# Turning two of four frame columns on VectorE by way of memory in a streaming encoder step

## The chip, the core and the metric

The kernel runs on one core of a Trainium2 chip. Its time is the device time of one execution in microseconds, from the first instruction to the last with what lies around them. A core has five engines that work side by side, each with a queue of its own: TensorE (PE in the profile; its weight loads are PEld), VectorE (DVE), ScalarE (ACT), GpSimd (POOL) and SyncE (SP), whose queue here issues most transfers. An engine works its queue in order, so an instruction that waits stops those behind it.

## What is computed

One layer of an encoder over 2048 new frames and 32 more frames of a running stream, 1024 wide. Cut to what matters:

```python
hn = rmsnorm(h, g_mix)
hA, bA, cA, zA, vB, zB = split(hn @ w_in)             # six times 512 columns
u  = cA * hA
yA = bA * (causal_conv3(u) + conv_b) * silu(zA)
pooled = trailing_mean(vB, windows 2, 4, 8, 16) - vB  # a window for each group of 128 channels
yB = (per_group(pooled) @ pool_w) * pool_scale * silu(zB)
h  = h + concat(yA, yB) @ w_out
gate = sigmoid(rmsnorm(h, g_ple) @ w_ple_gate)
y  = rmsnorm(h + (p @ w_ple) * gate, g_final)
```

`pool_w` has four matrices of 128 x 128, one for each group.

## The kernel before, in words

**Precision.** Every operand of a large product is kept as two parts, a high part (a copy to fp32r by ScalarE, L78) and a low part, the source minus the high part (VectorE, L79). `split` makes both. A product takes three matmuls for each block of the contraction: high by high, high by low, low by high.

**Frames.** The 2080 frames stand in five blocks of 416 (`NB`). Blocks 0 and 1 are the first group, 2 and 3 the second, 4 the third (`GROUPS`, L26). A block is cut into columns: three of 128 frames (c = 0, 1, 2) and one of 32 (c = 3). For a group of two blocks a column holds two tiles of 128 frames, or, for c = 3, one tile with 2 x 32 frames.

**Seven products for eight.** For two blocks and two weights at once the kernel forms sums and differences of the frames' quarters (names 11, 21, T1, T2, T3, 22, T4) and of the weights' quarters, and takes seven half products (`half_product`, L560) where eight would be due. A product is 12 matmuls of 128 x 416. `Unit.pair` (L859) issues the seven in order, in three PSUM banks X, Y and Z: product 1, 3, 5 and 7 in X, 2 in Y, 4 and 6 in Z. Between two products in one bank an engine takes the intermediate sum out: ScalarE by `carry` (L871), VectorE by `out` (L874). The fifth product's sum is taken by VectorE, and the seventh product then goes on in the same bank.

**Units.** A unit is a group and one of four blocks of 128 channels (`Unit`, L674). Units 0 to 3 belong to the first group, 4 to 7 to the second, 8 to 11 to the third. Unit 0 and the third group's units are computed plainly (`plain`, L777), the others with three pairs of weights: zb and v, c and h, za and b (`seven`, L899). v goes into the pooling mixer: `pool_blocks` (L731) takes the trailing mean, `mix` (L719) multiplies it with the unit's pooling weights (three matmuls per block, L724 to L726, into a PSUM bank). In `seven` the mix follows the second pair, in the third group it follows the product h directly.

**The second group's frames** are prepared while units 1 to 3 compute. `next_columns(3, 0, 1, 2)` (L1047) is a generator that does a column in small steps. `at_pace` (L1115) runs it beside the products: `aside` is called at each of the eight steps of a pair (24 times in a unit), and every call is worth 39/62 of a generator step. For a column `frame_sums` (L437) does this:

- the mean square of every tile, on ScalarE (`x_stat`, L397, L89), and the reciprocal root on GpSimd (L70, L74);
- the scaling of every tile with root and gain, one VectorE instruction a tile (`normal`, L404, L407);
- for each half of the 1024 rows, transposes on TensorE into a PSUM bank (`turn`, L411, L416), four for each tile. They are held in the written order;
- a copy of two of the quarters to SBUF by ScalarE (L452, L459), and four differences on VectorE (L449);
- for each of the seven names a `split` into a staging tile and a transfer to HBM from GpSimd's queue (`to_memory`, L483, L488).

When units 1 to 3 are done, `load_group` (L498, L502) brings the seven tiles of the second group back from HBM, seven transfers of 1664 KB.

**The last block** (block 4) takes another way (`last_block`, L1059), beside units 5 to 7. `scaled_to_memory` (L1091) scales a tile in four VectorE instructions, each writing 256 of 1024 columns in another order (L1098), and writes it to `xs_d` in HBM from GpSimd's queue (L1100). `from_memory` (L1102) reads it back in four transfers on SP's queue (L1106), each of which puts blocks of 32 frames on 32 partitions. `turned_in_place` (L1110) then transposes blocks of 32 x 32 in place, one VectorE instruction for the tile (L1112). After this the frames lie in the free dimension, as after a full transpose; TensorE takes no part.

**Rings.** Frame tiles, scaled tiles and staging tiles share the ring `xin`, five slots of 4 KB a partition (L337). The raw weights have the ring `raws`, four slots (L334). The pooling weights of all four groups are loaded once into a slot of that ring (L668, L669), and split once behind unit 0's first block (`vectors`, L656, L660).

**Order of the work.** A planner puts the instructions of each engine's queue in order by their place in the program and by its own estimate of when their inputs are ready. It may put a later instruction in front of an earlier one that would wait. `tc.keep_in_program_order` holds an instruction behind those that are written before it.

Of the kernel before, what the change touches and what calls it, by code (L numbers as in the profile page):

```python
# [9 lines left out]
F32 = mybir.dt.float32  # L10
F32R = mybir.dt.float32r
# [4 lines left out]
P = 128  # L16
D = 1024
# [13 lines left out]
LATE = 2  # L31
LATER = 4


@with_exitstack
def trunk(ctx, tc, x_p, x_s, c_conv, c_pool, p_p, p_s, g_mix, w_in, conv_w, conv_b, pool_w,
# [30 lines left out]
    def rstd_of(ssq, n, name, r=None):  # L67

        ms = sm.tile([P, 1], F32, tag="ms", name=f"ms_{name}")
        nc.gpsimd.tensor_scalar(ms[:n], ssq[:n], scalar1=1.0 / D, scalar2=EPS,  # L70
                                op0=ALU.mult, op1=ALU.add)
        if r is None:
            r = sm.tile([P, 1], F32, tag="rstd", name=f"rstd_{name}")
        nc.gpsimd.tensor_tensor(r[:n], ms[:n], nhalf[:n], op=ALU.pow)  # L74
        return r
# [255 lines left out]
    with ExitStack() as s1:  # L331
# [4 lines left out]
        frames_in = ExitStack()  # L336
        xin = frames_in.enter_context(tc.tile_pool(name="xin", bufs=5, side="right"))  # L337
        big = pool("big", 1)
# [134 lines left out]


        NAMES = ("11", "21", "T2", "T1", "T3", "22", "T4")
        SLOTS = (("11", "21"), ("T2", "T1"), ("T3", "22"))
# [6 lines left out]
        def to_memory(mem, name, src, at, n, t=None, later=False):  # L483
            t = t or staged(name)[:, :, :, :n]
            ins = put(t, src)
            if later:
                tc.keep_in_program_order(ins)
            nc.gpsimd.dma_start(mem[:, :, :, at:at + n], t.bitcast(F32))  # L488
# [156 lines left out]
        vec = const.tile([P, 112], F32, name="vec")  # L645
        pw = one.tile([P, 2, 4, P], F32R, name="pw")
        rows = ftile("rows").rearrange("p k n -> p (k n)")[:112, :P]
# [8 lines left out]
        def vectors():  # L656
            pv = tbank("pv")
            tc.keep_in_program_order(nc.tensor.transpose(pv[:, :112], rows, ident[:112, :112]))
            nc.vector.tensor_copy(vec, pv[:, :112])
            split(pw[:, 0], pw[:, 1], pw_raw)  # L660

# [5 lines left out]

        pw_raw = raws.tile([P, 4, P], F32, tag="t", name="raw_pw")  # L668
        nc.sync.dma_start(pw_raw, pool_w[0].rearrange("g c d -> c g d"))  # L669

# [3 lines left out]
        class Unit:  # L674


            def __init__(self, gi, tbs, j):
                self.gi, self.tbs, self.j, self.tag = gi, tbs, j, f"{gi}_{j}"
                self.L = min(SEQ - tbs[0] * NB, len(tbs) * NB)
                self.last = tbs[-1] == 4  # L680
                self.pooled = None
                t = lambda name, n: big.tile([P, n], F32, tag=name, name=f"{name}_{self.tag}")

                own = (gi, j) != (1, 0)
                self.zs = t("zs", 2 * NB) if own else ring4(xin, f"zs_{self.tag}")
                self.V = t("V", 2 * NB + 16)
                self.U = t("U", 2 * NB + 4)
                self.c_s = t("c_s", 2 * NB) if own else ring4(xin, f"c_s_{self.tag}")
                self.history(self.V, 15, halo_v, hist_v(j))
# [25 lines left out]
            def store(self, chunk, b, t):  # L715
                r = self.tbs[b] * NB
                nc.sync.dma_start(y_d[chunk, :, r:r + NB], self.cols(t, b))

            def mix(self, b):  # L719

                pp, j = self.cols(self.pooled.rearrange("p h n -> p (h n)"), b), self.j
                pq = self.pooled[:, 1, b * NB:b * NB + NB]
                pm = tbank(f"pm_{self.tag}_{b}")
                nc.tensor.matmul(pm[:, :NB], pw[:, 0, j], pp, start=True, stop=False)  # L724
                nc.tensor.matmul(pm[:, :NB], pw[:, 0, j], pq, start=False, stop=False)
                nc.tensor.matmul(pm[:, :NB], pw[:, 1, j], pp, start=False, stop=True)  # L726
                z = self.cols(self.zs, b)
                nc.vector.scalar_tensor_tensor(z, pm[:, :NB], pscale(j), z, op0=ALU.mult, op1=ALU.mult)
                self.store(4 + j, b, self.zs)
# [169 lines left out]
            def seven(self, B, aside, both=False):  # L899
# [54 lines left out]
                while i < 3:  # L954
# [4 lines left out]
                    for n in range(8):  # L959
# [3 lines left out]
                        if n == (0 if both else LATER):  # L963
                            while i and late:
                                tc.keep_in_program_order(split(*late.pop()))
                        if both and i == 2 and n == 3:
                            for b in range(2):
                                self.mix(b)
# [78 lines left out]
        def next_columns(*cs):  # L1047

            load_ahead(1, cs[0])
            for c, after in zip(cs, cs[1:] + (None,)):  # L1050

                places = iter(t[:, :, :, i * DEC:(i + 1) * DEC] for t in map(staged, ("short_0", "short_1")) for i in range(4))
                dst = lambda q, src, n: to_memory(p_d[q], f"{q}_1_{c}", src, c * P, n, next(places) if n == DEC else None, True)
                for i, _ in enumerate(frame_sums(ahead.pop((1, c)), f"g1_{c}", dst)):
                    if after is not None and i in (6, 7):
                        load_half_ahead(after)
                    yield
# [30 lines left out]

        xs_d = tc.dram_tile([NB, D], F32, name="xs_d")

# [37 lines left out]
        for gi, tbs in enumerate(GROUPS):  # L1128
# [17 lines left out]
            for j in range(4):  # L1146
                unit = gi * 4 + j
                u = Unit(gi, tbs, j)
                if unit == 0:
# [3 lines left out]
                    p_d["T4"] = tc.dram_tile([P, KH, 2, NB], F32, name="p_dT4b")  # L1153
                    aside = at_pace(next_columns(3, 0, 1, 2), 39, 62)
                elif gi == 0:
# [446 lines left out]
```

## Time and profile before

| | |
|---|---|
| median of three runs | 926.43 us (925.31 to 927.96) |
| profiled execution | 927.1 us |
| its span, first to last instruction | 925.3 us |
| mean granted clock of TensorE | 0.994 |
| instructions | 12917 |
| moved to and from HBM | 186.37 MB, mean 201 GB/s |

The profile is of a single execution on the chip. Its page gives, for each engine, the time in which it was busy; the span in 40 equal slices with the busy share of each in tenths; the transfers; and the costliest groups of instructions by line of the program, with the number of instructions, the mean duration, and what ended the idle time in front of them. The trace behind it also answers who waited for whom, and lists instructions in order of time. Instructions of one engine overlap, so that the distance between two starts says more of the cost of an instruction than its own duration. In the rows, `x12` is a number of instructions, `128x512 f32` partitions x elements and type, and `[0.87 <-DVE U L874]` an idle time of 0.87 us that ended with the VectorE instruction of line 874 on tile U.

### The profile page before, as it was taken

What the parts mean: (1) busy time and instruction counts of PE and PEld (TensorE: products, weight loads), DVE (VectorE), ACT (ScalarE), POOL (GpSimd) and SP (SyncE); (2) the same over time, 40 slices, a digit from 0 to 9 for tenths busy, and PEclk for the clock granted to TensorE, in tenths of its full rate; (3) what the DMA queues carried; (4) which work ended last, traced back from release to release, by engine and by line L of the source; (5) the groups of instructions that cost most, each with busy time, mean ns of one, the idle gap of its engine ahead of it and who ended that gap; (6) DMA issues with size and microseconds to landing.
All of it is one profiled execution on the core that took longest, in us unless ns stands there. A gap on an engine that the chain in (4) does not pass through costs nothing. (4 is left out here: it accounts for less than half of the span.)

```text
span 925.3 us, 12917 instructions
## 1 busy us (share of the span) xinstructions
PE 907.0 (98%) x4479; PEld 819.9 (89%) x4479; DVE 722.8 (78%) x1225; ACT 476.2 (51%) x880; POOL 152.8 (17%) x276
## 2 busy tenths in 40 slices
PE   7999999999999999999999999999999999999996
PEld 5999999999999999999999987888877868888884
DVE  6896898999488989785777679665554799888965
ACT  6744556554345455443545456334334776565554
POOL 3110222312001111000000010111111002333324
PEclk8999999999999999999999999999999999999998
DMA  8345555859955646357755359756775886799882
GB/s 245 87 152 153 167 160 178 265 154 317 411 165 174 191 155 189 100 180 277 201 169 173 125 192 289 263 186 177 251 220 167 292 259 160 190 232 232 227 240 91
DMA packets 140654, 186.37 MB, mean 201 GB/s; under 512 B 12044, under 2 KB 111244, under 8 KB 139309
## 3 DMA queue, kind: packets, MB, share of 16 engines
q1 hardware_dynamic: 120093, 126.07, 44.4%
q0 software_dynamic: 17760, 53.97, 19.8%
q10 hardware_dynamic: 2736, 5.51, 1.8%
q8 instruction: 35, 0.57, 0.3%
q14 instruction: 30, 0.25, 0.1%
HBM read 128.93 MB, written 56.56 MB: 200 GB/s over the span
## 5 line engine op out<-in xcount | busy, mean ns | idle before, releaser
L78 ACT CAST y_S<-y_fS 128x512 fp32r<-128x512 f32 x32 | 19.5, 621 | 41.9 <-PE x_o L168 18.9
L103 PE MATMUL e<-wq,pps 128*128 128x512 f32 (+1 forms) x156 | 38.9, 399 | 0.2 <-ACT pps L78 0.2
L168 PE MATMUL x_o<-wo_b,y_S 128*128 128x512 f32 x128 | 35.8, 391 | 0.0
L168 PE MATMUL x_g<-wg_b,g_S 128*128 128x512 f32 x128 | 35.7, 389 | 0.0
L564 PE MATMUL x_zbv<-B,w_zbv_S 128*128 128x416 f32 x168 | 34.2, 352 | 0.0
L564 PE MATMUL x_zab<-B,w_zab_S 128*128 128x416 f32 x168 | 34.1, 351 | 0.0
L564 PE MATMUL x_ch<-B,w_ch_S 128*128 128x416 f32 x168 | 34.1, 351 | 0.0
L564 PE MATMUL z_zab<-B,w_zab_S 128*128 128x416 f32 x168 | 34.0, 351 | 0.0
L564 PE MATMUL z_zbv<-B,w_zbv_S 128*128 128x416 f32 x168 | 34.0, 351 | 0.0
L564 PE MATMUL z_ch<-B,w_ch_S 128*128 128x416 f32 x168 | 34.0, 350 | 0.0
L103 PEld LDWEIGHTS e<-wq,pps 128*128 128x128 f32 (+1 forms) x156 | 27.4, 182 | 6.9 <-ACT pps L78 0.5
L1391 POOL DMA_DIRECT2D e<-h_d x28 | 24.8, 907 | 52.3 <-DVE e L1388 45.3
L70 POOL TENSOR_SCALAR ms_x<-ssq_x 128x1 f32<-128x1 f32 (+2 forms) x18 | 10.7, 592 | 127.5 <-ACT junk L89 127.2
L564 PEld LDWEIGHTS z_zbv<-B,w_zbv_S 128*128 128x128 f32 x168 | 31.4, 188 | 0.3
L564 PEld LDWEIGHTS z_zab<-B,w_zab_S 128*128 128x128 f32 x168 | 31.4, 188 | 0.3
L564 PEld LDWEIGHTS z_ch<-B,w_ch_S 128*128 128x128 f32 x168 | 31.4, 188 | 0.3
L564 PEld LDWEIGHTS x_zab<-B,w_zab_S 128*128 128x128 f32 x168 | 31.3, 188 | 0.4
L564 PEld LDWEIGHTS x_ch<-B,w_ch_S 128*128 128x128 f32 x168 | 31.3, 188 | 0.3
L564 PEld LDWEIGHTS x_zbv<-B,w_zbv_S 128*128 128x128 f32 x168 | 31.3, 188 | 0.4
L78 ACT CAST y<-y 128x512 fp32r<-128x512 f32 x24 | 14.8, 619 | 29.6 <-PE x_o L168 14.0
L168 PEld LDWEIGHTS x_o<-wo_b,y_S 128*128 128x128 f32 x128 | 23.9, 188 | 5.2 <-ACT c_o L1194 0.3
L168 PEld LDWEIGHTS x_g<-wg_b,g_S 128*128 128x128 f32 x128 | 24.0, 188 | 5.0
(582 smaller groups left out, 2649.9 us busy)
## 6 DMA issues: line engine op xcount, KB each, us to landing
y<-y_d SPq DMA_DIRECT2D x16, 512.0 KB, 6.3
x<-in_x_prompt_dram SPq DMA_DIRECT2D x16, 512.0 KB, 5.5
h_d<-x SPq DMA_DIRECT2D x16, 512.0 KB, 2.6
hn<-h_d SPq DMA_DIRECT2D x61, 128.0 KB, 6.7
xt<-in_x_prompt_dram SPq DMA_DIRECT2D x15, 512.0 KB, 7.4
e<-e_d SPq DMA_DIRECT2D x15, 512.0 KB, 5.9
e<-h_d POOLq DMA_DIRECT2D x28, 256.0 KB, 6.8
out_dram<-e POOLq DMA_DIRECT2D x14, 512.0 KB, 3.9
```

What stands on the lines that cost most here:

```text
L70: nc.gpsimd.tensor_scalar(ms[:n], ssq[:n], scalar1=1.0 / D, scalar2=EPS, op0=ALU.mult, op1=ALU.add)
L78: ins = nc.scalar.copy(hi, src)
L103: nc.tensor.matmul(ps[:n], pps[:, a, k, :n], wp[k][b][:, cs], start=k + q == 0, stop=k == 1 and q == 2)
L168: nc.tensor.matmul(ps[:n], lhs[:, k, a, :n], w[b][:, k], start=start and k + q == 0, stop=k == KH - 1 and q == 2, skip_group_check=True)
L564: nc.tensor.matmul(ps[:, :NB], lhs[:, k, x], b[:, k, y], start=start and k + q == 0, stop=stop and k == KH - 1 and q == 2, skip_group_chec ...
L1391: nc.gpsimd.dma_start(ee, h_d[r:r + P, at[1] * NH:at[1] * NH + NH], accum_op=ALU.add)
```

## The change

A new generator, `frame_blocks`, does for columns 3 and 0 what `frame_sums` does for a column; columns 1 and 2 keep `frame_sums`. It takes the last block's way: scaling in four pieces and a write to memory, four reads, one transpose in place. The quarters are then views of the transposed tile in SBUF, so the two ScalarE copies are not there, and the four differences and seven splits read SBUF. It has one step more than `frame_sums`, and the pace goes from 39/62 to 41/62 of a step a call. `xs_d` has rows for all these frames. The next column's two loads move from steps 6 and 7 to steps 8 and 9 (7 and 8 for column 3).

The ring `xin` gets a sixth slot of 4 KB. Pooling weights are loaded by every unit for its own group (128 x 128, in tiles of their own, one slot each), and split when the unit needs them: in `seven` behind the split of the pooled values, otherwise in `mix`. The tile of the mean square (`ms`) has four slots where it had eight.

```diff
+IN_BLOCKS = 3, 0
...
-        ms = sm.tile([P, 1], F32, tag="ms", name=f"ms_{name}")
+        ms = sm.tile([P, 1], F32, tag="ms", bufs=4, name=f"ms_{name}")
...
-        xin = frames_in.enter_context(tc.tile_pool(name="xin", bufs=5, side="right"))
+        xin = frames_in.enter_context(tc.tile_pool(name="xin", bufs=6, side="right"))
...
+        whole = lambda t: t.rearrange("p k (g t) -> p k g t", t=32)
+
+        def frame_blocks(xs, tag, rows, dst):
+            xs = [x_stat(x, True) for x in xs]
+            yield
+            for x, r in zip(xs, rows):
+                scaled_to_memory(x, r)
+                yield
+            ts = [from_memory(r, x[1]) for x, r in zip(xs, rows)]
+            yield
+            n = P if len(xs) == 2 else DEC
+            f1, f2, f3, f4 = (whole(ftile(f"f{c}_{tag}")[:, :, :n]) for c in range(1, 5))
+            sub = lambda o, x, y: nc.vector.tensor_tensor(o, x, y, op=ALU.subtract)
+            u = turned_in_place(ts[0])
+            p11, p21 = u[:, :KH, :n // DEC], u[:, KH:, :n // DEC]
+            dst("11", p11, n)
+            yield
+            if len(xs) == 2:
+                u = turned_in_place(ts[1])
+            else:
+                u = u[:, :, 1:]
+            p12, p22 = u[:, :KH], u[:, KH:]
+            sub(f1, p12, p11)
+            dst("T1", f1, n)
+            yield
+            sub(f2, p22, f1)
+            sub(f3, p22, p12)
+            dst("21", p21, n)
+            yield
+            sub(f4, p21, f2)
+            dst("22", p22, n)
+            yield
+            dst("T2", f2, n)
+            yield
+            dst("T3", f3, n)
+            yield
+            dst("T4", f4, n)
+            yield
...
-            ins = put(t, src)
+            v = whole if len(src.shape) == 4 else lambda a: a
+            ins = split(v(t[:, :, 0]), v(t[:, :, 1]), src)
...
-        pw = one.tile([P, 2, 4, P], F32R, name="pw")
...
-            split(pw[:, 0], pw[:, 1], pw_raw)
...
-        pw_raw = raws.tile([P, 4, P], F32, tag="t", name="raw_pw")
-        nc.sync.dma_start(pw_raw, pool_w[0].rearrange("g c d -> c g d"))
...
+                self.pw = one.tile([P, 2, P], F32R, tag="pw", name=f"pw_{self.tag}")
+                self.pw_raw = one.tile([P, P], F32, tag="pr", name=f"pr_{self.tag}")
+                nc.sync.dma_start(self.pw_raw, pool_w[0, j])
+                self.pw_whole = True
...
+            def pool_weights(self):
+                if self.pw_whole:
+                    self.pw_whole = False
+                    split(self.pw[:, 0], self.pw[:, 1], self.pw_raw)
+
             def mix(self, b):
+                self.pool_weights()
+                pw = self.pw
...
-                nc.tensor.matmul(pm[:, :NB], pw[:, 0, j], pp, start=True, stop=False)
+                nc.tensor.matmul(pm[:, :NB], pw[:, 0], pp, start=True, stop=False)
...
                                 tc.keep_in_program_order(split(*late.pop()))
+                                self.pool_weights()
...
-                for i, _ in enumerate(frame_sums(ahead.pop((1, c)), f"g1_{c}", dst)):
-                    if after is not None and i in (6, 7):
+                rows = (NB + c * P, 2 * NB + c * P) if c < 3 else (3 * NB,)
+                steps, loads = (frame_blocks(ahead.pop((1, c)), f"g1_{c}", rows, dst), (6 + len(rows), 7 + len(rows))) \
+                    if c in IN_BLOCKS else (frame_sums(ahead.pop((1, c)), f"g1_{c}", dst), (6, 7))
+                for i, _ in enumerate(steps):
+                    if after is not None and i in loads:
                         load_half_ahead(after)
...
-        xs_d = tc.dram_tile([NB, D], F32, name="xs_d")
+        xs_d = tc.dram_tile([4 * NB, D], F32, name="xs_d")
...
-                    aside = at_pace(next_columns(3, 0, 1, 2), 39, 62)
+                    aside = at_pace(next_columns(3, 0, 1, 2), 41, 62)
```

More of the change, by code (lines that the diff above doesn't have):

```diff
@@ L723, in mix @@
                 pm = tbank(f"pm_{self.tag}_{b}")
-                nc.tensor.matmul(pm[:, :NB], pw[:, 0, j], pp, start=True, stop=False)
-                nc.tensor.matmul(pm[:, :NB], pw[:, 0, j], pq, start=False, stop=False)
-                nc.tensor.matmul(pm[:, :NB], pw[:, 1, j], pp, start=False, stop=True)
+                nc.tensor.matmul(pm[:, :NB], pw[:, 0], pp, start=True, stop=False)
+                nc.tensor.matmul(pm[:, :NB], pw[:, 0], pq, start=False, stop=False)
+                nc.tensor.matmul(pm[:, :NB], pw[:, 1], pp, start=False, stop=True)
                 z = self.cols(self.zs, b)
```

## The prediction

> **What bounds the kernel now.** I read the busy times of the page first, then its forty slices, then the waits of TensorE in the stretch where the change acts, then the stretch unit by unit.
>
> ```profile
> span 925.3 us, 12917 instructions
> PE 907.0 (98%) x4479; PEld 819.9 (89%) x4479; DVE 722.8 (78%) x1225; ACT 476.2 (51%) x880; POOL 152.8 (17%) x276
> PE   7999999999999999999999999999999999999996
> DVE  6896898999488989785777679665554799888965
> ```
>
> TensorE (PE) is busy for 907.0 of 925.3 us, and only the first and last slices are not full. So a microsecond that TensorE no longer works is a microsecond of time, unless another engine makes it wait. The one with least room is VectorE (DVE): a slice is 23.1 us, and slices 4 to 10 (92 to 231 us), where the second group's frames are prepared, show 8 or 9 tenths.
>
> ```profile
> PE x_ch L564 <- DVE U L874: 0.9, 1, 0.9
> 78.47:129.26 50.79, 50.79 (x275) 49.52 (x275) 42.81 (x75) 27.48 (x55) 11.36 (x14) 1.00 0.49 147
> 129.26:181.84 52.58, 51.71 (x284) 50.61 (x283) 48.97 (x80) 30.54 (x58) 15.32 (x20) 1.00 0.78 240
> 181.84:232.66 50.82, 50.82 (x275) 49.74 (x274) 48.54 (x84) 26.93 (x50) 10.00 (x14) 1.00 0.76 235
> ```
>
> The first row is the only wait of TensorE between 40 and 320 us: 0.9 us for VectorE. The three others are units 1, 2 and 3 of the first group (stretch, its length, then busy us of PE, PEld, DVE, ACT, POOL, the granted clock, the DMA share, GB/s). VectorE works 42.81, 48.97 and 48.54 us in them: 140.3 of 154.2 us, 91%, with 13.9 us idle. The clock is 1.00, so nothing here is throttled.
>
> **What the change removes from TensorE.** Columns 3 and 0 lose their transposes on TensorE: 8 with 64 frames, 16 with 128. What a transpose costs is read from the starts of the products around it, not from its own duration, because instructions overlap. In the order of time (start, busy):
>
> ```profile
> 78.47 2.43 PE L564 MATMUL x_zbv<-B,w_zbv 128*128 128x416 f32 x12
> ...
> 87.63 0.46 PE L416 MATMUL pt_g<-ident,xt 64*128 64x64 f32 x4
> ...
> 95.02 0.46 PE L416 MATMUL pt_g<-ident,xt 64*128 64x64 f32 x4
> ...
> 97.78 2.43 PE L564 MATMUL y_ch<-B,w_ch 128*128 128x416 f32 x12
> ...
> 117.04 2.43 PE L564 MATMUL x_zab<-B,w_zab_S 128*128 128x416 f32 x12
> ...
> 121.58 1.04 PE L416 MATMUL pt_g<-ident,xt 128*128 128x128 f32 x8
> ...
> 124.72 2.43 PE L564 MATMUL z_zab<-B,w_zab_S 128*128 128x416 f32 x12
> 126.99 2.43 PE L564 MATMUL x_zab<-B_T,w_zab 128*128 128x416 f32 x12
> 129.26 1.03 PE L416 MATMUL pt_g<-ident,xt 128*128 128x128 f32 x8
> ...
> 132.40 2.43 PE L564 MATMUL y_zbv<-B,w_zbv 128*128 128x416 f32 x12
> ```
>
> A product of twelve matmuls starts 2.27 us after the one before it (124.72, 126.99, 129.26). From 117.04 to 132.40 there are six products, 13.62 us, and two sets of eight transposes: 15.36 - 13.62 = 1.74 us for column 0. From 78.47 to 97.78 there are eight products, 18.16 us, and column 3's two small sets: 19.31 - 18.16 = 1.15 us. Together **2.9 us** leave TensorE's own stream. Columns 1 and 2 keep theirs.
>
> ```profile
> L416 PE MATMUL pt_g<-ident,xt x56: 222/272/273, 87.6 to 199.4; 128*128 128x128 f32 x48, 64*128 64x64 f32 x8
> ```
>
> A single transpose has a duration of 272 ns, but eight cost 0.87 us, 0.11 us each: the rest lies beside neighbours. The Trainium skill (TensorE: Matmul & The Clock Gate, Part 4: PE-mode transpose) gives about 275 ns for a transpose inside a kernel. The trace has the same duration; a sum by it would take 24 times 0.275, an estimate of 6.6 us, off TensorE, and the spacing of the products speaks against that sum.
>
> **What it adds to VectorE.** These are the rows of what goes (L407, L459) and, from the last block, which already takes the way through memory, of what comes (L1098, L1112):
>
> ```profile
> L407 DVE SCALAR_TENSOR_TENSOR xt<-xt,rstd_x,g_bc 128x1024 f32<-128x1024 f32 (+1 forms) x14 | 18.0, 1283 | 9.6 <-POOL rstd_x L74 9.4 <-DVE g_bc L377 0.2
> 289.60 1.67 DVE L1098 SCALAR_TENSOR_TENSOR xs<-xt,rstd_x,g_bc 128x256 f32<-128x256 f32 x4 [0.73 <-POOL rstd_x L74]
> L1112 DVE STREAM_TRANSPOSE xb<-xb x4: 433/1232/1234, 303.6 to 380.2; 128x1024 f32<-128x1024 f32 x3, 128x256 f32<-128x256 f32 x1
> L459 ACT COPY f_g<-pt_g x4: 272/580/590, 95.5 to 200.5; 128x512 f32<-128x512 f32 x3, 128x128 f32<-128x128 f32 x1
> ```
>
> A full tile's scaling was one instruction of 1.28 us; it becomes four pieces, 1.67 us, and one transpose of 1.23 us. Column 0 has two tiles: 2 x (1.67 + 1.23 - 1.28) = 3.24 us. Column 3 has one tile of 64 rows: its pieces are as long per row, its transpose spans 512 elements, between 0.43 us (256) and 1.23 us (1024), so about 0.70 us by a straight line: 1.67 + 0.70 - 1.28 = 1.1 us. The four differences and seven splits of a column stay, as many and as wide, but read SBUF where they read PSUM; I take that as equal. So VectorE gets **4.3 us** more. ScalarE loses the two copies per column, 2 x 0.58 + 2 x 0.27 = 1.7 us; it has 40% idle here, so that is worth nothing.
>
> Pooling weights: one split of 512 columns becomes twelve of 128.
>
> ```profile
> L78 ACT CAST pw<-raw_pw x1: 622/622/622, 29.5 to 29.5; 128x512 fp32r<-128x512 f32 x1
> L79 DVE TENSOR_TENSOR pw<-raw_pw,pw x1: 680/680/680, 33.5 to 33.5; 128x512 fp32r<-128x512 f32 x1
> L79 DVE TENSOR_TENSOR short<-pt_g,short x3: 281/285/291, 89.6 to 100.2; 128x128 fp32r<-128x128 f32 x3
> 45.60 0.35 PE L724 MATMUL pm<-pp,pw 128*128 128x416 f32 x1
> ...
> 469.61 4.70 PE L564 MATMUL h<-hn,w_h 128*128 128x416 f32 x24
> 474.15 0.35 PE L724 MATMUL pm<-pp,pw 128*128 128x416 f32 x1
> ```
>
> Each costs VectorE 0.28 us, 0.84 us in units 1 to 3, and ScalarE about as much. In the third group TensorE goes from product h straight to the mix (474.15 is 4.54 us after 469.61), so a split that is done late would be seen. In the kernel before it was done 12 us ahead of the first mix (33.5 against 45.6 us); its inputs are in place a unit ahead, and both engines have gaps, so I cost it at nothing. If that cover is gone it costs up to 2.5 us a unit (a rival below).
>
> Put together: VectorE has 140.3 + 4.3 + 0.8 = 145.4 us of work in units 1 to 3, and these shrink to 154.2 - 2.9 = 151.3 us: 96% instead of 91%, 5.9 us idle instead of 13.9. It still fits, but only if nearly all of today's idle time can be used.
>
> **The way through memory, and the queues.**
>
> ```profile
> 291.56 0.60 POOL L1100 DMA_DIRECT2D xs_d<-xs  x1 [2.00 <-DVE xs L1098]
> 294.71 1.76 SPq L1106 DMA_DIRECT2D xb<-xs_d  x4
> xs_d<-xs POOLq DMA_DIRECT2D x3, 512.0 KB, 3.0
> xb<-xs_d SPq DMA_DIRECT2D x12, 128.0 KB, 2.7
> 100.36 0.37 SPq L514 DMA_DIRECT2D raw_zbv_2b<-in_w_in_dram  x1
> 108.95 0.68 DVE L542 TENSOR_TENSOR s_zbv<-raw_zbv_2b 128x512 f32<-128x512 f32 x1
> ```
>
> Three writes join POOL's queue, ahead of the next column's statistics, and twelve reads SP's. From the start of a tile's scaling to the tile back in SBUF: 1.67 + 0.60 + 3.0 + 1.76 + 2.7 = 9.7 us. A unit calls the generator 24 times in some 49 us and each call takes 41/62 of a step, so a step lasts 3.1 us. In column 0 the transpose stands three steps behind the scaling, 9.3 us: 0.4 us short. In column 3 it stands two steps behind, 6.2 us: 3.5 us short. The planner may put other ready work in front, but where it doesn't, a waiting transpose stops all of VectorE behind it: the sums that free PSUM banks (L874) and the low halves of weights (L79). On SP the reads wait for the write, with the next weights queued behind; such a weight tile was sent for at 100.36 and first read at 108.95, so a hold of some 4 us (the write's landing and its issue) stays hidden. The sixth ring slot lets loads start earlier, and TensorE waits for no such load today: nothing. DMA has a share of 0.49 in unit 1, where most of the extra transfers fall.
>
> The Trainium skill (SBUF — State Buffer, the warning on DVE blocking DMA) says that a DMA issued by GpSimd cannot get its descriptors while VectorE runs in a two-port mode; that would lengthen the write in this chain. The row above has 0.60 us for the issue and 3.0 us for the landing beside a busy VectorE, so the trace shows no such hold.
>
> **What I take for the new waits.** Their bounds: from below -1.0 us (today's one stall goes as well), from above everything that VectorE gains plus the two shortfalls, 4.3 + 0.8 + 3.9 = 9.0 us, if none is absorbed. The nearest row is that stall:
>
> ```profile
> 160.47 0.54 PE L564 MATMUL x_zab<-B,w_zab 128*128 128x416 f32 x2
> 161.89 2.55 PE L564 MATMUL x_ch<-B_T,w_ch 128*128 128x416 f32 x12 [0.87 <-DVE U L874]
> 161.26 0.58 DVE L874 TENSOR_TENSOR U<-x_ch,U 128x416 f32<-128x416 f32 x1
> ```
>
> The fifth product of a pair ends in bank X, VectorE must take it out (L874), and the seventh product needs the bank, one product later. So TensorE waits where VectorE is more than about 2 us late; here it was. Two matmuls (0.38 us) from 160.47 would have led to 160.85; the product started at 161.89, 1.0 us later. With VectorE at 96%, I take one more stall of this size: +0.9 us. The sum is -2.9 + 0.9 = **-2.0 us**. The profiled execution took 927.1 us, 1.8 of it outside the span, and lies 0.7 above the median of 926.4. Taken from the median: 924.4 us, 0.2% less. A measurement of this kernel can tell about 0.3%, 2.8 us, from no change, so the forecast is inside that.
>
> **The rivals.**
>
> ```profile
> DVE xt L407 <- POOL rstd_x L74: 4.8, 4, 3.4
> DVE w_zbv_S L79 <- ACT w_zbv_S L78: 3.8, 2, 2.3
> ```
>
> 1. Full gain. VectorE uses its idle time, and the stall at 161.9 stays or goes: -2.9 to -3.9 us, 923.5 to 922.5. For it: 8.6 us of VectorE's idle time between 60 and 240 us are waits for POOL and ScalarE (the rows above), which shrink by themselves when it runs late, and its weight work runs ahead (s_zbv at 108.95 is for a pair that starts at 130). Against it: today a stretch at 93% already gave a stall. Chance 0.30.
>
> 2. VectorE becomes the bound (the slower side). Place: units 1 and 2, at the sums from bank X. It decides where VectorE is over one product, 2.27 us, behind at such a sum; column 3's shortfall of 3.5 us alone does that. With half of the 9.0 us on the path: -2.9 + 4.5 = +1.6 us, 928.0; with all: +6.1 us, 932.5. For it: 96%, and the short way in column 3. Against it: 8.0 us of idle in unit 1, where column 3 and most of column 0 fall. Chance 0.22, half of it above +2.8 us.
>
> 3. The pooling split is left where it is written, behind the convolution. Then the mix in each of the third group's four units waits for VectorE's product and ScalarE's pass after h, some 2.5 us: -2.9 + 10.0 = +7.1 us, 933.5. Against it: the 12 us of lead. Chance 0.05.
>
> 4. Transposes cost their whole duration: 16 x 0.272 + 8 x 0.222 = 6.1 us, 920.3. The spacing of products speaks against it: 0.03. This is what the rule on transposes in the Trainium skill's TensorE page would come to.
>
> The forecast (-0.9 to -2.8 us) has 0.40.
>
> **How the numbers follow.** Faster by over 0.3%: rivals 1 and 4, 0.33. Slower by over 0.3%: rival 3, half of rival 2 and a little for the order of other work changing, 0.18. Within: 0.49. The range 922.4 to 929.0 takes in the forecast, rival 1 and the nearer half of rival 2; some 0.17 is left out. The forecast's own range is 923.6 to 925.5.
>
> **What would show it.** TensorE's transposes pt_g fall from 56 to 32, and products around columns 3 and 0 start 2.27 us apart; if TensorE's stream shortens by another amount than 2.9 us, the first term is wrong. VectorE's busy time in units 1 to 3 should be near 145 us. The waits of TensorE on VectorE (L874) before 235 us should add up to about 2 us; none means rival 1, over 5 means rival 2, with waits of the new transposes for the reads. A mix that waits for the low half of pw means rival 3. The prediction would be wrong most easily if the order of VectorE's queue elsewhere changed and stalls came or went in stages that the change doesn't touch.

## The result and the profile after

The changed kernel takes 938.21 us (median of five, 937.64 to 940.16) where the kernel before, on the same chip, takes 927.56 (925.31 to 927.96): a ratio of 1.0126 (of the means), 95% interval 1.0111 to 1.0142. It is slower by 1.3%, 10.7 us between the medians. The forecast was 924.4, with a range up to 929.0. The profiled execution took 940.16 us and was the slowest of the five. These are its span, its busy times, and TensorE's share and granted clock in forty slices:

```profile
span 938.4 us, 12956 instructions
PE 912.5 (97%) x4455; PEld 820.9 (87%) x4455; DVE 728.7 (78%) x1248; ACT 476.9 (51%) x887; POOL 153.4 (16%) x279
PE   7999998799999999999999999999999999999996
PEclk8999999899999999999999999999999999999998
```

The span is 13.1 us longer, while TensorE has 24 instructions fewer. TensorE's row has fallen in two slices, the seventh and eighth (141 to 188 us, 8 and 7 tenths), and the clock's in the eighth. The waits of TensorE between 100 and 260 us (us in total, times, longest), and then units 1, 2 and 3 (from the first product of a unit to that of the next, columns as in the prediction):

```profile
PE x_zab L610 <- DVE w_zab L80: 4.7, 1, 4.7
PE z_ch L610 <- ACT U L925: 2.2, 1, 2.2
PE x_ch L610 <- ACT c_s L925: 1.3, 1, 1.3
PE pt_g L417 <- DVE xt L408: 0.3, 1, 0.3
```

```profile
78.15:126.84 48.69, 48.69 (x259) 48.22 (x258) 42.93 (x84) 25.88 (x51) 11.72 (x16) 1.00 0.65 194
126.84:191.28 64.44, 55.89 (x275) 52.90 (x275) 53.35 (x86) 32.53 (x61) 16.11 (x21) 0.92 0.70 208
191.28:241.68 50.40, 50.40 (x276) 49.86 (x275) 48.33 (x83) 26.77 (x49) 10.09 (x15) 1.00 0.78 240
```

Unit 1 is 2.1 us shorter than before (48.69 against 50.79), unit 3 0.4 us shorter, and unit 2 11.9 us longer (64.44 against 52.58). VectorE is not full in unit 2: 53.35 of 64.44 us. Followed product by product, the second pair's third product starts at 147.22 where it started at 150.53: 3.3 us **ahead**. Unit 3 starts at 191.28 instead of 181.84: 9.4 us **behind**. So 12.7 us are lost in between. The four waits are 8.5 us, against 0.9 us in the kernel before. The rest, some 5 us, is for the most part a lower clock:

```profile
140.00:160.00 20.00, 16.18 (x82) 14.81 (x81) 15.12 (x26) 10.72 (x20) 6.87 (x10) 0.97 0.77 233
160.00:180.00 20.00, 15.27 (x66) 13.88 (x66) 18.11 (x29) 7.65 (x14) 2.58 (x3) 0.78 0.46 134
```

0.97 and 0.78 of the full clock over 20 us each are 0.6 + 4.4 = 5.0 us. In the kernel before, both stretches are at 1.00. In shorter stretches the clock is at half: 0.53 from 158.5 to 161.3, 0.50 from 161.4 to 162.0, and 0.50 from 173.5 to 178.5. From 171.0 to 173.5 (0.76) TensorE had no work, so 0.6 of the 5.0 us cost nothing: an estimate of 4.4 us for slower matmuls, and some 0.7 of the 12.7 us stay open. The clock's share also differs from one execution to the next. Two runs shown below with nearly the same waits (the one with 128 unused bytes and the one that reads back into the frame's own tile, 9.1 and 9.2 us) have 0.98 and 0.85, and 1.00 and 0.83, in these two stretches: 3.4 us each.

The chain that led there, from the changed kernel's timeline (start, duration, engine, instruction, and in brackets the idle time before it and what ended it):

```profile
144.93 2.91 SPq L394 DMA_DIRECT2D xt<-in_x_prompt_dram  x2
...
151.10 0.62 ACT L79 CAST T<-f_g 128x512 fp32r<-128x512 f32 x1 [3.05 <-DMA p_d<-21_1_0_1415]
...
152.68 0.48 ACT L925 COPY c_s<-x_ch 128x416 f32<-128x416 f32 x1
...
156.36 1.06 ACT L90 ACTIVATE junk<-xt 128x1024 bf16<-128x1024 f32 x1 [3.20 <-DMA xt<-in_x_prompt_dram]
...
157.42 0.49 ACT L925 COPY U<-z_ch 128x416 f32<-128x416 f32 x1
...
158.44 2.48 DVE L408 SCALAR_TENSOR_TENSOR xt<-xt,rstd_x,g_bc 128x1024 f32<-128x1024 f32 x2 [3.12 <-POOL rstd_x L75]
...
172.81 1.28 DVE L80 TENSOR_TENSOR w_zab<-raw_zab_2a,w_zab 128x512 fp32r<-128x512 f32 x2
...
173.54 3.84 PE L610 MATMUL x_zab<-B,w_zab 128*128 128x416 f32 x10 [4.73 <-DVE w_zab L80]
```

Read from the top: column 1's frames are asked for at 144.93. ScalarE, which has to keep the written order of these instructions, stops at 148 for a staging slot (the transfer of 21 has not landed), and at 153 for the second of the late frame tiles. Behind each stop stands a `carry` (c_s, U) that frees a PSUM bank, and TensorE waits for both. VectorE then scales column 1 from 158.44 on (from 149.85 in the kernel before), takes its quarters out, and only after these makes the low halves of w_zab, at 172.81. TensorE waits 4.73 us for them, and its next ten matmuls take 3.84 us (2.14 us for ten of them in the kernel before). The same places in the kernel before:

```profile
131.50 0.37 SPq L393 DMA_DIRECT2D xt<-in_x_prompt_dram  x1
136.30 0.76 SPq L393 DMA_DIRECT2D xt<-in_x_prompt_dram  x1
...
146.69 1.06 ACT L89 ACTIVATE junk<-xt 128x1024 bf16<-128x1024 f32 x1
...
155.27 0.51 ACT L871 COPY U<-z_ch 128x416 f32<-128x416 f32 x1 [1.76 <-PE z_ch L564]
155.39 1.28 DVE L79 TENSOR_TENSOR w_zab<-raw_zab_2a,w_zab 128x512 fp32r<-128x512 f32 x2
```

The first of the frames was asked for 13 us earlier, ScalarE waited for TensorE and not the other way round, and w_zab's low halves were made at 155.39.

A second, smaller loss lies where the change does nothing. From the first matmul of the embedding (e<-wp) to the last matmul the kernel before needs 374.65 us, the changed one 378.57: **3.9 us** more. No wait is new there; the matmuls themselves are longer (groups by line: number, busy us, mean ns), first in the changed kernel, then before:

```profile
L169 PE MATMUL x_o<-wo_b,y_S 128*128 128x512 f32 x128 | 36.4, 395 | 0.0
L169 PE MATMUL z_o<-wo_a,y_S 128*128 128x512 f32 x96 | 25.0, 395 | 0.0
L169 PE MATMUL x_o<-wo_T,y 128*128 128x512 f32 x96 | 23.1, 389 | 0.0
```

```profile
L168 PE MATMUL x_o<-wo_b,y_S 128*128 128x512 f32 x128 | 35.8, 391 | 0.0
L168 PE MATMUL z_o<-wo_a,y_S 128*128 128x512 f32 x96 | 24.4, 389 | 0.0
L168 PE MATMUL x_o<-wo_T,y 128*128 128x512 f32 x96 | 23.1, 389 | 0.0
```

So there are two questions: what stops ScalarE and VectorE in unit 2, and why do untouched matmuls take 1.5% longer.

### The profile page after: what moved, and what is told of

It is laid out like the page before. It is cut to its first block, busy times and chain, and to the rows that moved or that the text cites. A ratio compares the mean times of both kernels' runs of the same rounds, so it can differ in the third digit from the quotient of the medians.

```text
span 938.4 us, 12956 instructions
## 1 busy us (share of the span) xinstructions
PE 912.5 (97%) x4455; PEld 820.9 (87%) x4455; DVE 728.7 (78%) x1248; ACT 476.9 (51%) x887; POOL 153.4 (16%) x279
## 5 line engine op out<-in xcount | busy, mean ns | idle before, releaser
L79 ACT CAST y_S<-y_fS 128x512 fp32r<-128x512 f32 x32 | 19.5, 620 | 43.9 <-PE x_o L169 18.6
L79 ACT CAST y<-y 128x512 fp32r<-128x512 f32 x24 | 14.8, 618 | 29.6 <-PE x_o L169 14.4
```

Source lines behind the costliest of these rows:

```text
L79: ins = nc.scalar.copy(hi, src)
```

## The experiments

The letters stand for theories. **A**: column 1's frames come late; first because they are asked for two steps later, then because the ring has no free slot for them (**A2** says which slots). **B**: VectorE's added work. **C**: the addresses of the last stages' buffers. **D**: the timetable of steps alone. **Q**: the fixed order of VectorE's queue. The experiments ran on four chips, on which the kernel before had medians of 926.30 to 926.82 us (927.56 beside the changed kernel), so a difference between two of them is uncertain by about a microsecond.

### The loads' steps, and one column at a time

```diff
-    ... (frame_blocks(...), (6 + len(rows), 7 + len(rows)))
+    ... (frame_blocks(...), (6, 7))
```

> The changed kernel, with the next column's two loads back at steps 6 and 7 of a column (it had 8 and 9, and 7 and 8 for column 3). VectorE's work is the same. Theory A (column 1's frame tiles are asked for too late, and its statistics, held in order on ScalarE, then stop ScalarE, VectorE and TensorE): the stalls at 150 to 174 us mostly go, the time comes to 924 to 928 us. Theory B (VectorE is full, with 96% of the stretch): the stalls stay, 935 to 940 us.

936.93 us (933.06 to 937.23), ratio 1.0105 (1.0080 to 1.0131). The first form of A fails. The loads are issued as one group of two over 14.88 us:

```profile
131.10 14.88 SPq L394 DMA_DIRECT2D xt<-in_x_prompt_dram  x2
```

The first goes out as early as in the kernel before (131.10), the second is held on SP's queue for 13.5 us by column 0's last subtraction (L492). TensorE's waits stay, 4.9 us for w_zab and 2.0 us for c_s. The step at which a load is asked for is not what decides.

```diff
-IN_BLOCKS = 3, 0
+IN_BLOCKS = 3,
-    aside = at_pace(next_columns(3, 0, 1, 2), 41, 62)
+    aside = at_pace(next_columns(3, 0, 1, 2), 40, 62)
```

This is column 3 alone; the run after it has `IN_BLOCKS = 0,` at the same pace, and the third an empty `IN_BLOCKS` at 39 steps in 62.

> Only column 3 goes by way of memory (pace 40/62), column 0 as before; the ring of six and the split of pooling weights stay. Theory A: column 0 then holds no more slots than before, column 1's loads are at their old place, so only the gain of column 3 is left: 1.2 us below the kernel before, 925 to 927 us. Theory B: VectorE has only 1.1 us more, about the same, 926 to 928 us.

> Only column 0 goes by way of memory (pace 40/62), column 3 as before. Theory A: the loss hangs on column 0's six slots and its late loads alone, so it is all there: 936 to 940 us. Theory B: VectorE has 3.2 of the 4.3 us more, so about three quarters of the loss, 933 to 938 us. If it is below 929 us, both columns together are needed for the loss.

> No column goes by way of memory (pace 39/62 as before): only the ring of six, the pooling weights by unit, and the four slots of ms are left of the change. Both theories: no loss, 926 to 929 us. A time above 931 us would put a part of the loss on the pooling weights or on the ring.

| | us | ratio (95%) | third group starts | embedding starts | last matmul |
|---|---|---|---|---|---|
| before (its profile) | 926.82 | | 428.14 | 540.25 | 914.90 |
| column 3 alone | 930.18 | 1.0042 (1.0026 to 1.0058) | 425.16 | 536.49 | 917.04 |
| column 0 alone | 931.90 | 1.0061 (1.0044 to 1.0078) | 427.74 | 539.06 | 918.75 |
| neither | 928.46 | 1.0024 (1.0012 to 1.0037) | 429.62 | 540.94 | 919.60 |
| both | 938.21 | 1.0126 (1.0111 to 1.0142) | 437.07 | 549.07 | 927.64 |

The times are medians, the three starts are those of the profiled executions. Column 3 alone **gains** 3.8 us up to the embedding and yet ends 2.1 us later than the kernel before; with 930.18 it is outside both intervals given. Column 0 alone comes out about even up to the embedding, with one wait of 2.4 us for c_s, and is below both intervals. Only both together lose 9 us in the front part. And every row, the one with no column changed too, loses 4 to 6 us behind the embedding: 4 us of that come from what these kernels share. (The profiled execution with no column changed, 931.78 us, was the slowest of its nine; its median is 1.6 us above the kernel before.) The two runs with one column also have a new wait of 0.7 us for y (ScalarE, L79) there.

Column 0 alone says one thing more, on SP's queue:

```profile
SPq L394 <- DVE f_g L492: 9.6, 1, 9.6
```

There, too, column 1's frames wait for column 0's last subtraction; they are asked for at 140.11. But the low halves of w_zab are made at 159.77, ahead of column 1's tile 11, and TensorE doesn't wait for them. So late frames alone cost one wait of 2.4 us; the largest wait of the changed kernel needs the order of VectorE's queue as well.

### The addresses

`ms` with four slots instead of eight takes 128 bytes less of each partition, and everything that is placed behind it moves down by 128 bytes. The slots named wo_a, wo_b and wo_c lie at the other end of the memory and don't move.

```diff
-        ms = sm.tile([P, 1], F32, tag="ms", name=f"ms_{name}")
+        ms = sm.tile([P, 1], F32, tag="ms", bufs=4, name=f"ms_{name}")
```

> The kernel before, with nothing of the change but the ring of the norm's small `ms` tiles, 4 instead of 8; every buffer on the left side, the stationary tiles of the last two stages among them, so lies 128 bytes per partition lower, as in the changed kernel, while the slots that the matmuls stream from stay where they were. Theory C (the last stages, which the change does not touch, run slower because of the place of the buffers): 930 to 932 us, 4 to 5 us over the kernel before, the matmuls x_o<-wo_b and z_o<-wo_a at 394 to 396 ns instead of 389 to 391, the product stage up to the front part's end unchanged. Rival (the last stages are slower because of the order in which things arrive there, or the larger frame ring): within 1 us of the kernel before and matmuls at 389 to 391 ns.

930.13 us (927.46 to 932.65), ratio 1.0039 (1.0026 to 1.0052): a kernel that differs from the kernel before only in the size of a ring for single numbers is 3.5 us slower. Its third group starts at 427.88 (428.14 before), so nothing happens in the front part; from the embedding to the last matmul it needs 379.20 us. Its matmuls are those of the changed kernel:

```profile
L168 PE MATMUL x_o<-wo_b,y_S 128*128 128x512 f32 x128 | 36.4, 395 | 0.0
L168 PE MATMUL x_o<-wo_T,y 128*128 128x512 f32 x96 | 23.1, 389 | 0.0
```

The opposite edit puts the last stages' buffers back, in the changed kernel:

```diff
     with ExitStack() as s2:
+        gap = s2.enter_context(tc.tile_pool(name="gap", bufs=1)).tile([P, 32], F32, name="gap")
+        nc.gpsimd.memset(gap, 0.0)
```

> The changed kernel, with an unused tile of 128 bytes per partition ahead of the buffers of the last two stages, which puts them back at the addresses that they have in the kernel before. Theory C: 4 to 5 us under the changed kernel (933 to 934.5), matmuls x_o<-wo_b back at 391 ns or less, the stalls between 147 and 180 us unchanged (8 to 9 us of TensorE's waits). Rival (order of arrival): as the changed kernel, 937 to 939.

934.78 us (934.27 to 935.11), ratio 1.0094 (1.0080 to 1.0109): 3.4 us under the changed kernel where 4 to 5 were expected, with the waits in unit 2 unchanged (9.1 us). Its matmuls:

```profile
L169 PE MATMUL x_o<-wo_b,y_S 128*128 128x512 f32 x128 | 35.7, 390 | 0.0
L169 PE MATMUL x_o<-wo_T,y 128*128 128x512 f32 x96 | 23.6, 394 | 0.0
```

Now wo_T is the slow one. It is a weight that still lies 128 bytes lower, while the frames' side (y, y_S) is back in place. In the run before this one wo_T and y had moved together, and it was fast. So it is the **distance** between the two operands of a matmul that counts. Theory C stands, and its share of the 10.7 us is 3.4 to 3.9 us: 3.4 by this run, 3.5 by the one before, 3.9 by the two profiles.

### Slots, VectorE's work, or the timetable

```diff
-            ts = [from_memory(r, x[1]) for x, r in zip(xs, rows)]
+            ts = [from_memory(r, x[1], x[0]) for x, r in zip(xs, rows)]    # read back into the frame's own tile
```

> The changed kernel, with the block read back from memory put into the frame tile that it was scaled from, which is free by then, so that column 0 takes four slots of the frame ring instead of six and column 3 two instead of three. The work of every engine stays. Theory A (column 1's frames are asked for late because the ring has no free slot, and ScalarE, which takes its work in order, stops at them): column 1's loads go out by about 135 us, ScalarE's waits at junk<-xt (3.2 us) and TensorE's at c_s, U and w_zab (8.5 us together) go, 926 to 930 us. Theory B (VectorE's 4.3 us more do it): the waits stay within 2 us and the time is 935 to 938.

938.39 us (937.59 to 939.75), ratio 1.0134 (1.0120 to 1.0147): nothing gained. The waits of TensorE are the same, and on SP's queue:

```profile
SPq L394 <- DVE f_g L492: 14.5, 1, 14.5
```

This row stands in the changed kernel as well: column 1's first load waits 14.5 us for column 0's **last subtraction**. The ring hands its slots out in turn, to frame tiles, scaled tiles, tiles read back and staging tiles alike. A turned tile, in whichever slot, is read until the last subtraction, and column 1's load is given that slot. My edit saved slots, but not that one. In the kernel before, the quarters are in PSUM after the transposes, and the frame tiles are free at once.

```diff
                 normal(x)
+                for _ in range({"g1_3": 1, "g1_0": 2 - i}.get(tag, 0)):
+                    nc.vector.tensor_tensor(x[0][:x[1]], x[0][:x[1]], x[0][:x[1]], op=ALU.max)
```

> The kernel before, with idle work for VectorE in the frame columns and nothing else of the change: one more pass over a 128x1024 tile (the tile against itself, the larger value) in column 3, three in column 0, about 1.2 us each, so about 4.5 us in all, at the place of the scaling. Theory B (VectorE's added work makes the weights late): 5 to 9 us slower than before, with TensorE waiting for w_zab's low halves at about 170 us. Theory A (ring slots): within 1.5 us of the kernel before, since column 1's frames come as early as they did.

927.79 us (925.81 to 930.95), ratio 1.0018 (1.0003 to 1.0033). The four idle passes took 1.21 to 1.22 us each, 4.9 us together. They are paid with one wait of 2.5 us at column transposes, most of which is won back. Unit 3 starts at 182.17 (181.84 before) and the third group at 428.14, as before. VectorE's added work by itself costs about a microsecond, so theory B fails.

```diff
                 normal(x)
                 yield
+            if tag in ("g1_3", "g1_0"):
+                yield
...
-                    if after is not None and i in (6, 7):
+                    if after is not None and i in {3: (7, 8), 0: (8, 9)}.get(c, (6, 7)):
...
-    aside = at_pace(next_columns(3, 0, 1, 2), 39, 62)
+    aside = at_pace(next_columns(3, 0, 1, 2), 41, 62)
```

> The kernel before, with only the timetable of the change: one empty step more in columns 3 and 0 after the scaling, the next column's frames asked for at the steps at which the changed kernel asks, 41 steps in 62 instead of 39. No way through memory, no more work on any engine, ring of five. Theory D (column 0 simply runs some steps later and column 1 with it, and that alone stops ScalarE and TensorE): 5 to 9 us slower than before, with waits of TensorE for c_s, U or w_zab between 147 and 180 us. Theory A2 (the stop is the slots: the frame ring also holds the staging tiles, and a turned tile keeps its slot until the column's last subtraction): within 2 us of the kernel before.

926.93 us (925.56 to 929.60), ratio 1.0011 (1.0000 to 1.0022). The change's timetable without its slots costs nothing: theory D fails. What is left is A2, tried by the same operations in another order, and with the next column's loads at steps 6 and 7 again (which alone was worth 1.3 us, within the noise):

```diff
             dst("11", p11, n)
             yield
+            dst("21", p21, n)
+            yield
...
             sub(f1, p12, p11)
-            dst("T1", f1, n)
-            yield
             sub(f2, p22, f1)
             sub(f3, p22, p12)
-            dst("21", p21, n)
-            yield
             sub(f4, p21, f2)
             dst("22", p22, n)
             yield
+            dst("T1", f1, n)
+            yield
```

> The changed kernel with the same operations in another order inside a column that goes by way of memory: 11 and 21 are stored first, then the second tile is turned, all four subtractions follow at once and 22 is stored, so that both turned tiles are dead three steps earlier, and only then come T1 to T4; the next column's frames are asked for at steps 6 and 7. Theory A2: column 1's two loads go out by 142 us, ScalarE's waits at junk<-xt and at p_d's landing fall under 1 us each, TensorE's 8.5 us of waits fall under 3, and the time is 928 to 931 us (the last stages keep their 4 us of slower matmuls). Theory D: waits of 6 us or more remain, 934 to 938 us.

931.98 us (931.36 to 932.48), ratio 1.0058 (1.0046 to 1.0069): 6.2 us of the changed kernel's loss are gone, though the time is a microsecond over the interval that A2 gave. Column 1's loads now go out at 128.29 and by 139.8:

```profile
128.29 11.47 SPq L394 DMA_DIRECT2D xt<-in_x_prompt_dram  x2
```

ScalarE's stops and TensorE's waits for c_s and U are not there any more. The wait for w_zab stays, so 5.2 us of waits are left where under 3 were expected:

```profile
PE x_zab L610 <- DVE w_zab L80: 4.3, 1, 4.3
PE pt_g L417 <- DVE xt L408: 0.9, 1, 0.9
```

With the 128 bytes put back as well:

> The same order as in the run before, and the unused 128 bytes ahead of the last two stages' buffers. By theory A2 and theory C together: 3 to 4 us under the run before, 924.5 to 928 us, the best version that the experiments point to; by theory D with C: 930.5 to 934.5 us.

928.82 us (926.68 to 930.37), ratio 1.0023 (1.0013 to 1.0033), 3.2 us under the run before it, so the two causes add up. It is 0.8 us above the interval given, with the same wait of some 4 us left.

### The order of VectorE's queue

An engine's order is fixed when the program is made. At 41 steps in 62 the first two low halves of w_zab for unit 2 stand behind column 1's evictions and its tiles 11 and 21. In the compiled program of the changed kernel at 40 steps they stand behind 11 only, at 39, 42 and 43 ahead of both, as in the kernel before.

```diff
-    aside = at_pace(next_columns(3, 0, 1, 2), 41, 62)
+    aside = at_pace(next_columns(3, 0, 1, 2), 42, 62)
```

> The changed kernel with 42 steps in 62 instead of 41, nothing else; this puts w_zab's low halves of unit 2 ahead of column 1's evictions in VectorE's queue, where the changed kernel has them behind two of them. Theory Q (that wait is the order of VectorE's queue): the 4.7 us wait for w_zab goes, the waits for c_s and U (3.5 us), which are the slots', stay, 931 to 935 us. If the slots make the w_zab wait too, it stays at 3 us or more and the time is 936 to 939 us.

935.06 us (934.68 to 935.52), ratio 1.0089 (1.0076 to 1.0102). Half right: the wait for w_zab's low halves is gone, and so are those for c_s and U, which were to stay; two others took their place:

```profile
PE pt_g L417 <- DVE xt L408: 4.0, 1, 4.0
PE x_zab L610 <- DVE w_zab_S L80: 2.9, 1, 2.9
```

This edit isn't the order alone: column 1's frames are asked for at 138.97 instead of 144.93. They are still late, and the waits have mostly moved; the gain is 3.1 us. With the slots free early it is worth more. The next kernel has the reordered column and 42 steps in 62, and takes the 128 bytes up again ahead of all the buffers that had moved:

```diff
-        cnt = one.tile([P, first_of(4)], F32, name="cnt")
+        cnt = const.tile([P, first_of(4)], F32, name="cnt")
```

> The reordered column (11, 21, both tiles turned, all subtractions, 22, then T1 to T4; next frames at steps 6 and 7), 42 steps in 62, and a small table of counts moved from one pool to another so that every buffer of the last two stages lies where it does in the kernel before. If slots, queue order and addresses are the whole loss: no wait of TensorE over 1 us between 60 and 260 us, matmuls x_o<-wo_b, z_o<-wo_a and x_o<-wo_T at 389 to 391 ns, 921.5 to 925.5 us, 1 to 5 us under the kernel before. If something else of the change costs time: 926 us or more.

**923.01 us** (922.52 to 924.56), ratio **0.9963** (0.9951 to 0.9974): faster than both kernels, by 3.6 us and by 15.2. What is left of the waits between 60 and 260 us, the clock in the stretch where it had fallen to 0.78, and the matmuls:

```profile
PE x_zab L610 <- DVE w_zab_S L80: 1.2, 1, 1.2
```

```profile
160.00:180.00 20.00, 18.84 (x99) 18.16 (x99) 19.70 (x33) 13.00 (x26) 6.19 (x9) 1.00 0.93 281
```

```profile
L169 PE MATMUL x_o<-wo_b,y_S 128*128 128x512 f32 x128 | 35.8, 391 | 0.0
L169 PE MATMUL x_o<-wo_T,y 128*128 128x512 f32 x96 | 23.1, 389 | 0.0
```

One wait of 1.2 us is left where less than 1 was expected. VectorE works 19.70 of 20 us in that stretch, and that does no harm.

> Column 3 alone by way of memory (40 steps in 62), with the same move of the small table, so at the addresses of the kernel before. The run with column 3 alone took 930.2 us with its front part 3.8 us ahead and 5.6 us given back in the last two stages. Theory C: the 5.6 us are kept but for 0.5, 924.5 to 927 us. Rival (the last stages lose because the front part is ahead): 929 to 931 us.

This is the run with column 3 alone and the same move of `cnt`. 927.04 us (925.46 to 929.58), ratio 1.0006 (0.9996 to 1.0016): no difference from the kernel before, 3.1 us better than at the shifted addresses, just past the upper end of what theory C gave. Column 3 by itself is 2.2 us ahead at the embedding and gives 1.7 us of it back later: 0.7 us in a wait of x_o for y (ScalarE, L79) that the kernel before doesn't have; the rest I did not find.

## Why the prediction was wrong

**TensorE's gain was right.** The products from 78 to 147 us were to lose 2.9 us of transposes; the changed kernel is 0.3 us ahead at 78.15 and 3.3 us at 147.22, 3.0 us for 24 transposes. The estimate of 6.6 us by the duration in the Trainium skill (TensorE: Matmul & The Clock Gate, Part 4) would have been more than twice that; here the measurement decides.

**VectorE's work was right, and its being the bound was not the danger.** 145.4 us were forecast for units 1 to 3, 144.6 are measured (42.93 + 53.35 + 48.33). The idle passes show that this much work costs about 1 us. Rival 2 had the right place, unit 2, but its highest price, 932.5, was still 6 us short, and its mechanism was another: VectorE was idle for 11 of unit 2's 64 us, waiting in its order, and none of TensorE's four waits is for a sum that VectorE takes out of bank X.

**The way through memory did not stop VectorE.** No new transpose waits for its reads. The planner put column 0's first one 14 us behind the start of the scaling, where I had counted 9.3, so the 9.7 us fitted:

```profile
118.18 3.25 DVE L1156 SCALAR_TENSOR_TENSOR xs<-xt,rstd_x,g_bc 128x256 f32<-128x256 f32 x8
...
132.20 1.23 DVE L1170 STREAM_TRANSPOSE xb<-xb 128x1024 f32<-128x1024 f32 x1
```

The pooling split (rival 3) shows no wait of a mix for it.

**The step that failed is "The sixth ring slot lets loads start earlier, and TensorE waits for no such load today: nothing".** I counted slots added and not how long they are held. A column by way of memory takes twice the slots of frame tiles (scaled and read back), and the turned ones live to the last subtraction, where they had been free after the transposes. One more slot did not pay for that: column 1's frames were asked for up to 13 us later, ScalarE stopped in order behind them and behind a staging slot, and TensorE behind ScalarE. With the slots free early, these waits (c_s and U, 3.5 us) are gone.

**The last term, the new waits at +0.9 us, failed with it**: 8.5 us of waits were measured, and behind them 5.0 us by the granted clock that no term had. The largest wait, 4.7 us for w_zab, has a cause of its own besides the late frames. VectorE's queue had its low halves behind column 1's tiles: with the frames early it was still 4.3 us, and in the other order it was gone. The prediction thought of a change in that queue's order only in stages that the change doesn't touch, and gave it no price. The term's bound of 9.0 us was made from VectorE's work and the shortfalls; it held neither the ring, nor the queue's order, nor the clock. The clock gate is told in the Trainium skill (TensorE: Matmul & The Clock Gate, Part 1): one idle window of about 3.4 us takes the clock to half. The trace agrees in kind behind the wait of 4.73 us: the twenty matmuls from 173.54 to 179.96 needed 6.42 us where they need 3.78 at the spacing of 2.27 us for twelve. It also shows the clock at half from about 158.6 to 162.0, where no single wait before had reached 3.4 us (1.29 and 2.22). In the run that reads back into the frame's own tile, the clock stayed at 1.00 from 150 to 170 us at nearly the same waits. So the lengths of the waits alone don't give the loss.

**The second failure is of the same step about rings.** I took `ms` as free. It moved operands of the last stages by 128 bytes and cost 3.4 to 3.9 us there. The prediction named stages that the change does not touch as its weakest place, but looked for stalls there, not for longer matmuls. A slip of its own: its chances outside the range add up to 0.19, not 0.17.

**The sum, as the runs have it:** reordering for the slots 6.2 us, the addresses 3.2, 42 steps in 62, which changes the queue's order (with wo_T's address), 5.8; together 15.2 us, from 938.2 to 923.0. What then stands against the kernel before, 3.6 us faster, lies in what rival 1 gave for the case without new waits, 922.5 to 923.5. That is in part luck: it is more than that, 4.9 us, ahead at the third group's start, and loses some of it later. The three shares are not independent: the 42 steps alone gave 3.1 us. Open is why that version is only 2.5 us ahead at the embedding; its mixes wait 1.1 us for pooled values there, the rest I have not traced.

## What to carry to other kernels

When a tile moves from PSUM to a ring in SBUF, write down for each slot which instruction reads it last, and who gets the slot next; a ring with one more slot can be the tighter one. Before an edit of a buffer's size is costed at nothing, look at which later buffers it shifts, and compare durations of the same matmuls before and after. Look also at where VectorE's fixed order has put the next weights. And add the clock to the price of a wait: here 8.5 us of waits brought an estimated 4.4 us of slower products behind them, in other runs less.

## What the runs showed of the hardware

In the groups shown, matmuls of 128 x 512 took 389 to 391 ns with the operands' starts a multiple of 2,048 bytes apart in a partition (in the compiled program wo_b lies at 202,720, the frames' tiles from 96,224 on in steps of 4,096), and 394 to 396 ns with one of them 128 bytes lower; moving both left 389. It holds in both directions (128 bytes off in the run with `ms` alone, back with the gap), and for wo_T in the opposite one. Two groups don't fit as well: x_o<-wo_a,y_S took 401 ns in the kernel before and 404 after, and z_o<-wo_d,y_S, whose two operands both moved, went from 389 to 392. The product matmuls of 128 x 416 in the front part show no such cost: there the same shift left the third group's start within 0.3 us. Which other distances are slow was not tried.
